# Three 64-byte-row loads ahead of the first store, and that store in one DMA instead of two

## The chip, the cores and the metric

The kernel runs on one core of one Trainium2 chip. The metric is the device time of an execution in microseconds (us). Before the change the median of three runs is 314.12 us (314.10 to 314.14).

## What is computed

Two arrays are woven into one along the last axis, in 32-bit floats. Each input has 32 x 256 x 1024 elements (33.55 MB), the output twice that (67.11 MB).

```python
result = np.zeros((batch, seq, dim * 2), dtype=np.float32)
result[..., 0::2] = x
result[..., 1::2] = y
```

Nothing is computed on the values. All 134.22 MB have to pass through the core's 16 DMA engines once: 67.11 MB are read and 67.11 MB are written.

## The kernel before, in words

`x` and `y` are cut into n = 8 tiles each, numbered k. A tile is 128 partitions (rows of the on-chip memory) by W = 8192 elements, so a row is 32 KiB and a tile is 4 MiB. The output tile k is twice as wide; it is written in two halves h = 0 and 1, each again 128 rows of 32 KiB, from a buffer of its own. Below, "store [k,h]" is the DMA of half h of tile k. There are two buffers each for x (`xt`), for y (`yt`) and for the output halves (`ot`).

Four parts run side by side and meet at semaphores:

- **Loads**, on the queue of SyncE (SP): x0 in two halves (the second half goes out on the other queue, L46), then y0, x1, y1, x2, y2 and so on (L45 to L55). From k = 2 on, the load of x into a buffer waits until VectorE has copied the x of tile k-2 out of it (L50), and the load of y the same for y (L54).
- **Weaving**, on VectorE (DVE): per half, one copy puts half a tile of x into the even elements of `ot[h]` (L67) and one copy puts y into the odd ones (L70). The x copy waits for the load of x and, through `osem[h]` (L66), for the store that last used `ot[h]`. The first y copy of a tile waits for the load of y. Each copy raises `woven` by one.
- **Stores**, on the queue of ScalarE (ACT): when both copies of a half are done (L74), the half goes out (L76). Store [0,0] alone is cut in two by `parts` (L39): its first quarter goes as 128 rows of 8 KiB, the rest as 128 rows of 24 KiB. `stored` (L42) counts the increments that `osem` has then got. ACT does nothing else but issue these.
- **The end**: ACT waits for the last store of half 0 and clears the semaphores (L80, L83); SP waits for the last store of half 1 (L84).

A DMA is spread over the 16 DMA engines; with 128 rows each engine gets 8 of them. Each engine keeps the rows of the two queues apart, and adds to each DMA's rows a packet of 4 bytes that raises the semaphore. `tile_interleave_kernel` moves the first DMA of either queue into the program's opening; that touches the two halves of x0 only.

Of the kernel before, what the change touches and what calls it, by code (L numbers as in the profile page):

```python
# [3 lines left out]


def _interleave(nc, x, y, out):
    P = 128
    W = 8192
    H = W // 2  # L10

    total = 1
    for s in x.shape:
        total *= s
    n = total // (P * W)
    assert n * P * W == total

    def rows(ap, names, k):
        flat = ap.rearrange("b s d -> (b s d)")
        return flat[k * names : (k + 1) * names].rearrange("(p w) -> p w", p=P)  # L20

    fp32 = mybir.dt.float32
    xt = [nc.alloc_sbuf_tensor(f"xt{b}", [P, W], fp32).ap() for b in (0, 1)]
    yt = [nc.alloc_sbuf_tensor(f"yt{b}", [P, W], fp32).ap() for b in (0, 1)]
    ot = [nc.alloc_sbuf_tensor(f"ot{b}", [P, W], fp32).ap() for b in (0, 1)]

    xsem = [nc.alloc_semaphore(f"xsem{b}") for b in (0, 1)]
    hsem = nc.alloc_semaphore("hsem")
    ysem = [nc.alloc_semaphore(f"ysem{b}") for b in (0, 1)]
    woven = nc.alloc_semaphore("woven")  # L30
    osem = [nc.alloc_semaphore(f"osem{b}") for b in (0, 1)]

    xs = [rows(x, P * W, k) for k in range(n)]
    ys = [rows(y, P * W, k) for k in range(n)]
    os_ = [rows(out, 2 * P * W, k) for k in range(n)]

    Q = W // 4

    def parts(k, h):  # L39
        return [slice(0, W)] if k or h else [slice(0, Q), slice(Q, W)]  # L40

    def stored(k, h):  # L42
        return 16 * sum(len(parts(j, h)) for j in range(k))

    nc.sync.dma_start(out=xt[0][:, :H], in_=xs[0][:, :H]).then_inc(xsem[0], 16)  # L45
    nc.scalar.dma_start(out=xt[0][:, H:], in_=xs[0][:, H:]).then_inc(hsem, 16)  # L46
    for k in range(n):
        b = k % 2
        if k >= 2:
            nc.sync.wait_ge(woven, 4 * (k - 2) + 3)  # L50
        if k:
            nc.sync.dma_start(out=xt[b], in_=xs[k]).then_inc(xsem[b], 16)
        if k >= 2:
            nc.sync.wait_ge(woven, 4 * (k - 2) + 4)  # L54
        nc.sync.dma_start(out=yt[b], in_=ys[k]).then_inc(ysem[b], 16)  # L55

    for k in range(n):
        b = k % 2
        for h in (0, 1):
            c = slice(h * H, (h + 1) * H)  # L60
            if h == 0:
                nc.vector.wait_ge(xsem[b], 16 * (k // 2 + 1))
            elif k == 0:
                nc.vector.wait_ge(hsem, 16)
            if k:
                nc.vector.wait_ge(osem[h], stored(k, h))  # L66
            nc.vector.tensor_copy(out=ot[h][:, 0::2], in_=xt[b][:, c]).then_inc(woven, 1)  # L67
            if h == 0:
                nc.vector.wait_ge(ysem[b], 16 * (k // 2 + 1))
            nc.vector.tensor_copy(out=ot[h][:, 1::2], in_=yt[b][:, c]).then_inc(woven, 1)  # L70

    for k in range(n):
        for h in (0, 1):
            nc.scalar.wait_ge(woven, 4 * k + 2 * h + 2)  # L74
            for c in parts(k, h):
                nc.scalar.dma_start(  # L76
                    out=os_[k][:, h * W : (h + 1) * W][:, c], in_=ot[h][:, c]
                ).then_inc(osem[h], 16)

    nc.scalar.wait_ge(osem[0], stored(n, 0))  # L80
    used = sorted(s.num for s in [*xsem, hsem, *ysem, woven, osem[0]])
    assert used == list(range(used[0], used[-1] + 1)), used
    nc.scalar.sem_clear(range(used[0], used[-1] + 1))  # L83
    nc.sync.nop(nofuse=True).wait_op(osem[1], stored(n, 1), "sem-ge").then_inc(  # L84
        osem[1], -stored(n, 1)
    )


def kernel(tc, x, y, out):
    nc = tc.nc  # L90
    tc.close()
    tc.compile()

    _interleave(nc, x, y, out)

    blocks = nc.main_func.blocks
    for engine in (mybir.EngineType.SP, mybir.EngineType.Activation):
        opening = blocks[0].instructions
        at, moved = next(
            (b, i)  # L100
            for b in blocks[1:]
            for i in b.instructions
            if i.engine == engine and i.opcode == "DMACopy"
        )
        assert not (moved.sync_info and moved.sync_info.on_wait)
        body = at.instructions
        body.remove(moved)
        gate = next(
            n
            for n, i in enumerate(opening)  # L110
            if i.engine == engine and i.opcode == "Drain"
        )
        opening.insert(gate, moved)
        at.instructions = body
        blocks[0].instructions = opening


# [1 line left out]
_INS = ['x', 'y']  # L119
_OUTS = [((32, 256, 2048), 'float32')]  # L120


# [23 lines left out]
```

## Time and profile before

| | |
|---|---|
| median of the runs | 314.12 us |
| the profiled execution | 314.21 us |
| its span, from the first to the last instruction | 312.9 us |
| read and written | 67.11 MB and 67.11 MB, 429 GB/s over the span |
| packets | 4896, of which 544 are under 512 bytes (34 DMAs x 16 engines) |
| DMA queue of ACT (q10), of SP (q1) | 51.3% and 48.5% of the 16 engines' span |
| VectorE busy | 71.9 us (23%), 32 copies of some 2.29 us |
| issue of the first store | at 24.35 us |
| landing of store [0,0] | first DMA at 40.41 us, second at 57.50 us |
| last load lands | 277.78 us |
| last four stores land | 283.80, 293.49, 303.18 and 312.85 us |

The profile is of one execution. The span leaves 1.33 us outside the first and the last instruction. The profile's page names the queue of SP q1 and that of ACT q10. "Share of 16 engines" is the time that the packets of a queue took, against 16 times the length of the span or of the stretch that was asked for; the two queues' shares together show how full the DMA engines were. A landing is the moment at which the last of the 16 engines has raised the DMA's semaphore. The trace also holds a record of each packet: its start, its length, its size and its queue, but not its engine.

### The profile page before, as it was taken

How to read it: one execution, taken by the hardware profiler on the slowest of the kernel's cores; microseconds unless marked ns; L12 is line 12 of the kernel's file. 1: busy time of each engine (PE TensorE's matmuls, PEld its weight loads, DVE VectorE, ACT ScalarE, POOL GpSimd, SP SyncE). 2: the span in 40 equal slices, each digit the busy share in tenths (PEclk: the TensorE clock that was granted, in tenths of full speed). 3: DMA queues.
4: the chain of work that ended last, by engine and by line, in shares of the span. 5: the costliest groups of instructions: out<-in, count | busy, mean ns of one | idle time of the engine just before them, and what ended most of it. 6: DMA issues, size and time to landing. Idle time of an engine off the chain costs nothing.

```text
span 312.9 us, 114 instructions
## 1 busy us (share of the span) xinstructions
DVE 71.9 (23%) x32; POOL 0.2 (0%) x4
## 2 busy tenths in 40 slices
DVE  0216000501305023050230503205032050415400
POOL 0000000000000000000000000000000000000000
DMA  8999999999999999999999999999999999999998
GB/s 344 461 406 431 436 402 431 440 465 406 448 423 431 440 406 465 402 469 402 469 402 465 406 457 415 436 436 419 452 402 469 402 469 402 469 402 461 411 444 360
DMA packets 4896, 134.22 MB, mean 429 GB/s; under 512 B 544, under 2 KB 544, under 8 KB 544
## 3 DMA queue, kind: packets, MB, share of 16 engines
q10 hardware_dynamic: 2592, 69.21, 51.3%
q1 hardware_dynamic: 2304, 65.01, 48.5%
HBM read 67.11 MB, written 67.11 MB: 429 GB/s over the span
## 4 chain that ended last, share of the span: by engine, by line
DMA 82%; DVE 12%; issue 0%
DMA out_dram<-ot 76%; DMA yt<-in_y_dram 7%; DVE ot L70 6%; DVE ot L67 6%
## 5 line engine op out<-in xcount | busy, mean ns | idle before, releaser
L67 DVE COPY ot<-xt 128x4096 f32<-128x4096 f32 x16 | 36.7, 2295 | 218.0 <-DMA out_dram<-ot 206.3
L70 DVE COPY ot<-yt 128x4096 f32<-128x4096 f32 x16 | 36.6, 2288 | 8.0 <-DMA yt<-in_y_dram 8.0
L130 POOL MEMSET const-uint8-127<- 128x1 uint8 x1 | 0.1, 102 | 0.0
L130 POOL MEMSET const-bfloat16-1.0<- 128x1 bf16 x1 | 0.1, 101 | 0.0
L130 POOL MEMSET const-float32-0.0<- 128x1 f32 x1 | 0.1, 98 | 0.2 <-issue 0.2
L130 POOL MEMSET const-float32-1.0<- 128x1 f32 x1 | 0.1, 98 | 0.0
## 6 DMA issues: line engine op xcount, KB each, us to landing
out_dram<-ot ACTq DMA_DIRECT2D x15, 4096.0 KB, 34.1
yt<-in_y_dram SPq DMA_DIRECT2D x8, 4096.0 KB, 41.5
xt<-in_x_dram SPq DMA_DIRECT2D x7, 4096.0 KB, 24.4
out_dram<-ot ACTq DMA_DIRECT2D x1, 3072.0 KB, 32.8
xt<-in_x_dram SPq DMA_DIRECT2D x1, 2048.0 KB, 11.7
xt<-in_x_dram ACTq DMA_DIRECT2D x1, 2048.0 KB, 13.4
out_dram<-ot ACTq DMA_DIRECT2D x1, 1024.0 KB, 16.1
```

The costliest lines, as they stand in the source:

```text
L67: nc.vector.tensor_copy(out=ot[h][:, 0::2], in_=xt[b][:, c]).then_inc(woven, 1)
L70: nc.vector.tensor_copy(out=ot[h][:, 1::2], in_=yt[b][:, c]).then_inc(woven, 1)
L130: nc = _bacc.Bacc("TRN2", target_bir_lowering=False, num_devices=1)
```

## The change

Store [0,0] becomes one DMA with rows of 32 KiB, as all others are. Ahead of it, on the same queue and behind the same wait for the first two copies, ACT issues three loads of 4, 8 and 12 rows of 64 bytes from the start of x into a spare tile that nobody reads. They raise a semaphore of their own, `tsem`, for which ACT waits at the end. The increments in `osem` are counted without the extra part.

```diff
+    spare = nc.alloc_sbuf_tensor("spare", [12, 48], fp32).ap()
...
+    tsem = nc.alloc_semaphore("tsem")
...
-    def parts(k, h):
-        return [slice(0, W)] if k or h else [slice(0, Q), slice(Q, W)]
-
-    def stored(k, h):
-        return 16 * sum(len(parts(j, h)) for j in range(k))
...
-                nc.vector.wait_ge(osem[h], stored(k, h))
+                nc.vector.wait_ge(osem[h], 16 * k)
...
-            for c in parts(k, h):
-                nc.scalar.dma_start(
-                    out=os_[k][:, h * W : (h + 1) * W][:, c], in_=ot[h][:, c]
-                ).then_inc(osem[h], 16)
+            if k == h == 0:
+                for r in (4, 8, 12):
+                    nc.scalar.dma_start(
+                        out=spare[:r, slice(4 * r - 16, 4 * r)],
+                        in_=xs[0][:r, slice(4 * r - 16, 4 * r)],
+                    ).then_inc(tsem, 16)
+            nc.scalar.dma_start(
+                out=os_[k][:, h * W : (h + 1) * W], in_=ot[h]
+            ).then_inc(osem[h], 16)
...
+    nc.scalar.wait_ge(tsem, 48)
```

More of the change, by code (lines that the diff above doesn't have):

```diff
@@ L35, in _interleave @@
     os_ = [rows(out, 2 * P * W, k) for k in range(n)]
-    Q = W // 4
-    def parts(k, h):
-        return [slice(0, W)] if k or h else [slice(0, Q), slice(Q, W)]
-    def stored(k, h):
-        return 16 * sum(len(parts(j, h)) for j in range(k))
     nc.sync.dma_start(out=xt[0][:, :H], in_=xs[0][:, :H]).then_inc(xsem[0], 16)
@@ L74, in _interleave @@
             nc.scalar.wait_ge(woven, 4 * k + 2 * h + 2)
-            for c in parts(k, h):
-                nc.scalar.dma_start(
-                    out=os_[k][:, h * W : (h + 1) * W][:, c], in_=ot[h][:, c]
-                ).then_inc(osem[h], 16)
-    nc.scalar.wait_ge(osem[0], stored(n, 0))
-    used = sorted(s.num for s in [*xsem, hsem, *ysem, woven, osem[0]])
+            if k == h == 0:
[8 more added lines that the diff above has]
+    nc.scalar.wait_ge(tsem, 48)
+    nc.scalar.wait_ge(osem[0], 16 * n)
+    used = sorted(s.num for s in [*xsem, hsem, tsem, *ysem, woven, osem[0]])
     assert used == list(range(used[0], used[-1] + 1)), used
     nc.scalar.sem_clear(range(used[0], used[-1] + 1))
-    nc.sync.nop(nofuse=True).wait_op(osem[1], stored(n, 1), "sem-ge").then_inc(
-        osem[1], -stored(n, 1)
+    nc.sync.nop(nofuse=True).wait_op(osem[1], 16 * n, "sem-ge").then_inc(
+        osem[1], -16 * n
     )
```

## The prediction

> **What bounds the kernel.** I read the page first, then the rate stage by stage, then the packet records around the first store.
>
> The slices of the page and its chain of waits:
>
> ```profile
> DMA  8999999999999999999999999999999999999998
> DMA packets 4896, 134.22 MB, mean 429 GB/s; under 512 B 544, under 2 KB 544, under 8 KB 544
> ...
> DMA 82%; DVE 12%; issue 0%
> ```
>
> The DMA engines are full in every slice but the first and the last. The chain names VectorE for 12%, but only because it follows waits: the digits show that the DMA engines stay busy while VectorE copies. The bound is therefore not the chain but the 16 engines' throughput. The table by stretches says how flat it is, with one whole period of the loop per line (start and end, length, VectorE, GpSimd, clock, DMA share, GB/s):
>
> ```profile
> 77.00:115.70 38.70, 8.96 (x5) 0.00 (x0) 1.00 1.00 434
> 115.70:154.40 38.70, 8.97 (x5) 0.00 (x0) 1.00 1.00 434
> 154.40:193.20 38.80, 9.06 (x5) 0.00 (x0) 1.00 1.00 432
> ```
>
> Per engine a period is 32 rows of 32 KiB. The packet records give 1213 ns for nearly each of them, load or store; 32 x 1.213 = 38.8 us. So the middle cannot be quickened by another order of the same rows. Time is lost only where an engine has no row, or a row takes over 1213 ns.
>
> There are two such places. The start: the first packet begins at 1.00 us and the first 16 take 1.27 us on average where later ones of their size take 0.61. The change does not touch it. The other is where the stores begin. The DMA view of two stretches, 13.5 to 26.9 us (loads alone) and then 27.0 to 32.1 us (first store rows):
>
> ```profile
> q1 hardware_dynamic: 192, 5.77, 99.6%
> ```
> ```profile
> q1 hardware_dynamic: 48, 1.57, 80.6%
> q10 hardware_dynamic: 42, 0.34, 15.9%
> ```
>
> In the first, 0.996 x 13.4 us x 16 engines over 176 rows (16 of the 192 are 4-byte packets) is 1.213 us a row; in the second, 0.806 x 5.1 x 16 / 48 = 1.371 us. Three load rows per engine are each 0.158 us too long: **0.47 us lost per engine**. It ends at 32.2 us; from 60 us on nothing of the kind comes back.
>
> How an engine shares itself between the queues is seen from 28.45 to 40.85 us, while store [0,0] sends its 8 KiB rows:
>
> ```profile
> DMA packets 288, 5.24 MB, mean 423 GB/s; under 512 B 32, under 2 KB 32, under 8 KB 32
> ...
> q1 hardware_dynamic: 144, 4.19, 81.4%
> q10 hardware_dynamic: 144, 1.05, 20.0%
> ```
>
> Both queues got 144 packets, 9 per engine: 8 rows and one 4-byte packet each. The engine changes queue after every packet, whatever its size, and the 4-byte packet (9 ns) uses a turn. Whoever sends short packets lets the other queue go ahead.
>
> **The change, part by part.** Times are against the profiled execution, 314.21 us, span 312.9.
>
> *The split goes.* A row pair cost 309 + 912 = 1221 ns; one row of 32 KiB costs 1213. That is 8 ns x 8 rows, and one completion packet of 9 ns less: **-0.07 us** per engine. It counts in full, since every engine is full to the end. On ACT one issue of 0.34 us goes.
>
> *What the split did to the order goes too.* It cost the store queue 9 more turns, so loads ran ahead. Now loads get fewer rows before the stores become equal. At 28.5 us, when the first store row started, an engine had 22 of its 128 load rows done. Alternating from there (106 pairs of 2.426 us) it ends its loads at 285 us (sem packets and the later start move that up to 288) instead of 277. Some 22 store rows then remain, 22 x 1.213 = 26.7 us, which is the same end: 312. Order changes, sums do not.
>
> *Three loads come.* Each engine that gets a row of such a load has two more packets per load on the store queue (row and completion), so two turns in which a 32 KiB load row passes. With one row per engine, the engine that takes part in all three sees 6 turns, 6 x 1.213 = 7.3 us; engines that take part in none go on at once. The stores of some engines thus run up to 7.3 us behind, and their loads as far ahead. By the section "Why a DMA increments its semaphore by 16 and not by 1" of the Trainium skill's page "DMA: Bandwidth & Descriptors", 4, 8 and 12 rows go to the 4, 8 and 12 lowest engines, which would give lags of 6, 4, 2 and 0 turns; the trace has DMAs of 128 rows only, all with 16 completions, and cannot show it.
>
> Their own time: 64 bytes lie between the rows of 4 bytes (9 ns) and 8 KiB (309 ns). The records fall nearly on a line (309, 611, 1213), so I take 9 ns: 6 x 9 = **+0.05 us** on the engine with all three. From below it cannot be less than nothing. From above, a packet whose read is not fetched ahead: the first 16 rows took 0.66 us more than later ones on average, at most 0.97 (1.58 against 0.61); 3 x 0.97 = +2.9 us. I take the low end, because the nearest case is the second half of x0, the first load on the ACT queue beside a running SP queue: its first 16 rows took 619 to 721 ns against 611, so the read of a first packet is fetched while another packet runs.
>
> *Issues on ACT.* Three more at 0.34 to 0.46 us put the first store off by about 1.1 us (24.35 to 25.4). Store [0,1] waits for copies that end at 28.7, so nothing else moves. The cover is x1 and y1, 10 load rows per engine at 28.5 us; without it 1.1 us would be lost.
>
> *Does an engine run dry?* Store [0,0] lands on the lagging engine at about 28.5 + 7.3 + 8 x 2.426 = 55.2 us (before: 57.50). y1 lands on the leading one about 52 to 55. Copies (4.5 us) end near 60, and store [1,0] goes out. The engines furthest ahead still have [0,1] until 29.7 + 16 x 2.426 = 68.5. From issue to first packet the first store took 28.5 - 24.35 = 4.1 us, so 4 us are to spare, and a dry store queue would only let loads pass. In the last stretch both matter: [6,1] ends with 16 rows left, 312.5 - 19.4 = 293.1. y7 lands at 285 to 288, its copy (2.3 us) lets [7,0] go at 287 to 290.3; that leaves 2.8 us or more, where the fastest issue to first packet is 1.0 (first load). By then loads are over on all engines and the lag is made up.
>
> *The 0.47 us at the first stores.* Not explained by the trace. Bounds: it goes (-0.47), or it lasts for the six extra load rounds as well (6 x 0.158 = +0.95). I take 0, the row as it is.
>
> *The added wait on `tsem`* stands at the end of ACT, long after those loads. Nothing.
>
> Sum: 314.21 - 0.07 + 0.05 = 314.19. The median of the runs lies 0.09 below the profiled execution, so the forecast is **314.1 us**.
>
> **Against it: the fixed cost of a DMA.** The last rows in store order end at 303.18 and 312.85 us with 9.67 us between them, 8 x 1.213 = 9.70: no gap between one DMA and the next. The same page ("Anatomy of one DMA") gives about 2 us of fixed cost per DMA, which for two more DMAs would be an estimated +4 us, 318; the trace shows that cost hidden behind the other rows, so the rule stands only beside the third rival.
>
> **The rivals.**
> 1. *The loss at the first stores disappears* because the engines no longer begin together: 314.19 - 0.47 - 0.09 = 313.6. For it: it sits in a lockstep start. Against: lockstep rows from 33 us on lose nothing. Chance 0.12, of which 0.05 reaches past -0.2%.
> 2. *It lasts or grows* with the longer staggered start: up to 315.0. Chance 0.08, half of it past +0.2%.
> 3. *The small loads are not hidden* (the slower side). Place: the engine with all three; each read makes the store queue's turn idle for 0.66 to 0.97 us: 2.0 to 2.9, so 316 to 317. It decides from 0.2 us each, since every delay of a full engine shows at the end. Chance 0.08.
> 4. *The rows of one small load go to one engine*: 24 rows and 3 completions, 27 turns, 33 us of lag there. Store [0,0] would land near 80 us; the others have 26 load and 16 store rows from 28.5 us on, until 79.5, and idle until [1,0] goes out about 87: some +8, 322. It decides when the lag exceeds the 16 store rows' slack. Chance 0.03.
> 5. *The margin before [7,0] is lost*, as with the 4.1 us of the first store against 2.8: +1.3, 315.4. Chance 0.03.
>
> **How the numbers follow.** The forecast has 0.66. A difference under 0.2% (0.63 us) is what a measurement of this kernel can tell from no change. Faster: 0.05 from rival 1 and 0.02 from elsewhere, 0.07. Slower: 0.04 + 0.08 + 0.03 + 0.03, 0.18. The same: 0.75. The range takes in the ends of rivals 1 and 2, 313.5 to 315.2; rivals 3, 4 and 5, 0.14 together, lie above it.
>
> **What would show it.** Packets 4896 - 144 + 48 = 4800, under 512 bytes 544 - 16 + 48 = 576; the periods still at 434 GB/s. Store [0,0] lands at 52 to 57 us; the completions of one DMA spread over some 7 us instead of 0.34 until the loads end, then join again. The last load at 285 to 288. Rows over 1213 ns around 28 to 36 us tell rivals 1 and 2; a DMA share under 1.00 between 280 and 300 tells 5; a hole around 80 us tells 4. The forecast is wrong if an engine shows a gap anywhere after 36 us.

## The result: slower by 0.34%

The changed kernel takes 315.11 us in the median of 6 runs (314.85 to 315.99), the kernel before 314.13 (314.10 to 314.29). The ratio is 1.0034, with a 95% interval of 1.0022 to 1.0046. The time lies inside the forecast's range (313.5 to 315.2), but the forecast was "no change" with 0.75, and "slower" had 0.18. It also varies more from run to run than before: over 1.1 us instead of 0.2. In the ratios below, executions more than 1.5% above the fastest of their kernel are left out (one each of e4 and e9); the medians hold them.

The profiled execution took 314.86 us with a span of 313.5 us (before: 314.21 and 312.9). The slices, the packets and the chain of its page:

```profile
DMA  8999999999999999999999999999999999999997
GB/s 337 466 401 418 401 451 406 464 406 464 406 460 406 464 406 464 406 464 406 456 414 452 418 451 418 435 435 414 456 406 464 406 460 406 464 406 464 406 464 339
DMA packets 4800, 134.22 MB, mean 428 GB/s; under 512 B 576, under 2 KB 576, under 8 KB 576
...
DMA 82%; DVE 12%; issue 0%
```

The page hardly differs: the same full slices, the same chain. 4800 packets with 576 small ones are what the change asks for. Three whole periods in the middle (stretch, length, VectorE, GpSimd, clock, DMA share, GB/s):

```profile
73.60:112.30 38.70, 8.99 (x4) 0.00 (x0) 1.00 1.00 434
112.30:151.00 38.70, 8.99 (x4) 0.00 (x0) 1.00 1.00 434
151.00:189.70 38.70, 8.99 (x4) 0.00 (x0) 1.00 1.00 433
```

Nothing was lost there either. What is left is the beginning of the stores. The DMA view from 27.0 to 32.1 us, the stretch that showed 80.6% and 15.9% before:

```profile
q1 hardware_dynamic: 67, 1.84, 99.7%
q10 hardware_dynamic: 47, 0.23, 10.9%
```

The shares sum to over 100% because rows that run past the stretch count whole, so the rows have to be read one by one. The packet records carry no engine, but rows follow one another without a gap and each engine gets a known number of packets from each DMA, so the records can be strung into 16 sequences. In each I sum by how much rows exceed their usual length (1213 ns for 32 KiB, 309 for 8, 611 for 16, 912 for 24) from 20 us on. I call that the engine's **loss**. Before: 0.53 us on average, 0.32 to 0.68. After: 0.92 on average, **0.58 to 1.23**. Single load rows between 28.5 and 33 us take up to 2193 ns.

The loss has become larger, and also unequal. That is seen at the end, where each engine's last packet raises a semaphore. The DMA view from 312.6 us on, first of the kernel before, then of the changed one:

```profile
DMA packets 0, 0.00 MB, mean 0 GB/s; under 512 B 0, under 2 KB 0, under 8 KB 0
```
```profile
DMA packets 15, 0.00 MB, mean 0 GB/s; under 512 B 15, under 2 KB 15, under 8 KB 15
```

Before, all engines are done by then (312.17 to 312.50 us); after, 15 of 16 still have their last packet to send (312.52 to 313.16). The time of the kernel is that of the last engine, plus 1.70 us in nearly every profile of this study.

### The profile page after: what moved, and what is told of

It is laid out like the page before. It is cut to its first block, busy times and chain, and to the rows that moved or that the text cites. A ratio compares the mean times of both kernels' runs of the same rounds, so it can differ in the third digit from the quotient of the medians.

```text
span 313.5 us, 117 instructions
## 1 busy us (share of the span) xinstructions
DVE 72.0 (23%) x32; POOL 0.2 (0%) x4
## 4 chain that ended last, share of the span: by engine, by line
DMA 82%; DVE 12%; issue 0%
DMA out_dram<-ot 76%; DMA yt<-in_y_dram 7%; DVE ot L65 6%; DVE ot L62 6%
## 6 DMA issues: line engine op xcount, KB each, us to landing
xt<-in_x_dram ACTq DMA_DIRECT2D x1, 2048.0 KB, 13.5
```

## The experiments

All times are medians. What a kernel is "above before" is its distance from the kernel before measured beside it on the same chip, 314.20 to 314.24 us; the row "before" is of the comparison above. Loss and last end are of the one profiled execution, whose time is in the fourth column.

| kernel | median (runs) | ratio, 95% interval | profiled | loss: mean, most | last engine ends |
|---|---|---|---|---|---|
| before | 314.13 | | 314.21 | 0.53, 0.68 | 312.50 |
| after | 315.11 (6) | 1.0034, 1.0022 to 1.0046 | 314.86 | 0.92, 1.23 | 313.16 |
| e1 unsplit, no small loads | 314.47 (11) | 1.0008, 0.9999 to 1.0016 | 314.52 | 0.86, 1.09 | 312.82 |
| e2 split and small loads | 316.29 (6) | 1.0064, 1.0042 to 1.0087 | 314.94 | 0.93, 1.30 | 313.25 |
| e3 early touch | 316.54 (5) | 1.0070, 1.0057 to 1.0083 | 317.04 | 2.00, 3.57 | 315.34 |
| e4 x2 and y2 held | 317.44 (6) | 1.0096, 1.0074 to 1.0118 | 317.88 | 1.81, 4.42 | 316.16 |
| e5 all sixteen | 314.49 (12) | 1.0005, 0.9995 to 1.0015 | 314.43 | 0.73, 0.85 | 312.73 |
| e6 small loads early | 314.25 (12) | 0.9996, 0.9986 to 1.0006 | 314.29 | 0.60, 0.88 | 312.60 |
| e7 small loads mid | 314.21 (12) | 0.9998, 0.9990 to 1.0006 | 314.22 | 0.53, 0.82 | 312.51 |
| e8 one of eight | 315.15 (11) | 1.0035, 1.0021 to 1.0049 | 317.14 | 1.81, 3.35 | 315.43 |
| e9 small loads second | 321.62 (6) | 1.0232, 1.0189 to 1.0275 | 325.07 | 3.28, 11.31 | 323.36 |
| e10 large part first | 314.40 (11) | 1.0005, 0.9996 to 1.0013 | 314.40 | 0.55, 1.04 | 312.69 |
| e11 two halves | 314.42 (11) | 1.0006, 0.9997 to 1.0015 | 314.40 | 0.60, 0.77 | 312.71 |
| e12 three-part ramp | 315.09 (11) | 1.0029, 1.0017 to 1.0040 | 315.46 | 0.59, 1.82 | 313.76 |
| e13 mended | 318.88 (6) | 1.0148, 1.0115 to 1.0181 | 317.55 | 1.67, 4.03 | 315.84 |
| e14 sixteen, second | 314.53 (11) | 1.0012, 1.0003 to 1.0021 | 314.53 | 0.72, 0.84 | 312.83 |
| e15 after, second profile | 315.06 (1) | | 315.06 | 0.96, 1.38 | 313.23 |
| e16 after, third profile | 315.61 (1) | | 315.61 | 1.16, 2.22 | 313.77 |

**Which part of the change.** e1 drops the small loads, e2 puts them into the kernel before.

```diff
# e1, against the changed kernel
-            if k == h == 0:
-                for r in (4, 8, 12):
...
# e2, against the kernel before
             nc.scalar.wait_ge(woven, 4 * k + 2 * h + 2)
+            if k == h == 0:
+                for r in (4, 8, 12):
...
```

> The changed kernel without the three small loads: store [0,0] is one DMA of 32 KiB rows, all engines begin it together. Theory A (the small loads are to blame: they make the engines begin to store one group after the other, and the loads that still run are slowed for as long as that lasts): 314.0 to 314.2 us as before, loss between 26 and 40 us about 0.5 us per engine. Theory B (the longer rows of the first store are to blame, the small loads are innocent): 314.9 to 315.2, loss about 0.9. If both count, something between.

> The kernel before with the three small loads ahead of its two-part first store. Theory A: 314.8 to 315.2 us, with the loss around the first stores at 0.9 us. Theory B: 314.1 to 314.3 us, loss 0.5.

e1 is 0.23 us above before, and its interval just reaches no change; e2 is 2.05 us above. The small loads count far more than the split. In e1 all engines lose more than before (0.67 to 1.09). Two kernels further down that also begin with an unsplit store in step, e5 and e14, are 0.29 and 0.32 us above with a mean loss of 0.73, and e14's interval excludes no change; so the unsplit store most likely costs some 0.2 to 0.3 us. How far the loss accounts for it is open: e9, the same as e1 up to its second store, lost only 0.53 before 50 us.

In these four the loss has a place. All their rows that are over 0.03 us too long before 50 us are load rows that begin before any engine's first store row: in e1 the store is issued at 24.21 us, the long rows begin from 25.81 to 27.87, the first store row at 29.1.

Whether the split also harms beside the small loads is not shown. The intervals of e2 and of the changed kernel overlap, and the profile of e2 is of its fastest execution. It has no load row from 81.4 to 86.9 us: its load queue ran dry, as that of the changed kernel never did before the loads ended.

**What the loss is not.** e3 writes to the output early; e4 issues fewer DMAs near the first store.

```diff
# e3
+    nc.scalar.wait_ge(xsem[0], 16)
+    nc.scalar.dma_start(out=os_[0][:, :16], in_=xt[0][:, :16]).then_inc(wsem, 16)
+    nc.scalar.wait_ge(wsem, 16)
...
# e4
             nc.sync.wait_ge(woven, 4 * (k - 2) + 3)
+            if k == 2:
+                nc.sync.wait_ge(osem[0], 16)
```

> The changed kernel; in addition 128 rows of 64 bytes go from the first x tile to the 128 rows of the first output tile as soon as x0's first half is there (some 12 us), and the first store overwrites them. Theory C (the loss comes with the first write to the output, whoever makes it): the loss moves to some 13 to 17 us or goes, and there is none at 28 to 36 us; if it goes, 314.1 us or below. Theories A and B: loss and time as in the changed kernel, 314.9 to 315.5.

> The changed kernel; SP issues the loads of x2 and y2 only after store [0,0] has landed (some 54 us), so that fewer DMAs are issued from 24 to 29 us. Theory D (the loss comes from the many DMA issues in those microseconds): the loss at 28 to 36 us shrinks to under 0.4 us per engine, 314.2 to 314.5. Theories A, B and C: loss about 0.9, 314.9 to 315.5. The queue of SP may be empty for a moment near 54 us, which costs nothing while stores run.

In e3 no row is too long from 12 to 27 us, while the early rows are written, and from 27 to 36 us an engine loses 0.76 us on average. In e4 it is 0.89 there, in the changed kernel 0.90. The first write (theory C) and the burst of issues (theory D) are out. Both kernels turned out slower by losses further on. In e3, whose first store goes out 1.0 us later, the eight engines with two or three small loads lose another 1.4 to 2.6 us each after 60 us, the others at most 0.9. In e4 the four engines with two small loads have store rows up to 1.25 us too long at 40 to 46 us and, as the held loads begin, at 55 to 58; they lose 4.2 to 4.4 us in all, the others up to 1.4. e4 also shows what the prediction's fifth rival would look like. Its timeline near the end:

```profile
282.71 2.29 DVE L64 COPY ot<-xt 128x4096 f32<-128x4096 f32 x1 [14.93 <-DMA out_dram<-ot]
292.34 2.29 DVE L67 COPY ot<-yt 128x4096 f32<-128x4096 f32 x1 [7.33 <-DMA yt<-in_y_dram]
294.67 7.38 ACTq L78 DMA_DIRECT2D out_dram<-ot  x2
```

y7 comes late, store [7,0] goes out at 294.67 us, its first rows start at 295.51, and twelve engines stand still for 1.8 to 2.4 us. In the changed kernel the same copy ends at 289.27 us, and [6,1] lands at 293.50 to 294.17: no gap.

**Together or in groups.** e5 gives every engine the same extra turns; e6 and e7 put the small loads elsewhere; e8 keeps one load, so two groups 2 turns apart.

```diff
# e5, against the changed kernel
-                        out=spare[:r, ...], in_=xs[0][:r, ...]
+                        out=spare[:16, ...], in_=xs[0][:16, ...]
# e6, against the kernel before: the three loads right behind the load of x0's second half
# e7, against the kernel before
+            if k == 3 and h == 0:
+                for r in (4, 8, 12):
...
# e8, against the changed kernel
-                for r in (4, 8, 12):
+                for r in (8,):
```

> The changed kernel with 16 rows in each of the three small loads, so that all engines get the same 6 extra turns and begin to store together, as much later as the last ones in the changed kernel. Theory A (staggering costs): the completions of a store lie within 0.7 us, time as in the unsplit kernel without small loads, 0.1 to 0.4 us above the kernel before. Theory F (six more turns at the start of the stores cost, whoever has them): 0.9 us or more above it, as in the changed kernel.

> The kernel before, with the three small loads right behind the second half of x0 on the ACT queue, about 12 us before any store is ready. The stagger is then gone before the stores begin, since the ACT queue is empty from some 20 us on. Theory A: within 0.15 us of the kernel before. If the small loads cost by themselves (reads of 64 bytes, issues, three more completions): 0.5 us or more above it.

> The kernel before, with the three small loads ahead of store [3,0] (issued near 139 us) instead of the first store. Theory A in its wide form (engines out of step cost whenever they fall out of step): no loss before 140 us beyond that of the kernel before, rows over 1213 ns behind it, 0.4 us or more above the kernel before. Theory G (only the beginning of the stores is touchy, a stagger later is free): within 0.15 us of the kernel before.

> The changed kernel with the load of 8 rows alone: two groups of engines, 2 turns (2.4 us) apart, instead of four groups over 6 turns. Theory A: between the unsplit kernel without small loads and the changed kernel, 0.3 to 0.8 us above the kernel before. Theory F: one third of the changed kernel's surplus. If two groups cost as much as four, the size of the stagger is not what counts.

e5 carries 48 small rows instead of 24 and is 0.29 us above before, no worse than e1 without any. e6 is 0.05 above. So neither the small loads nor the extra turns cost anything that these runs can tell: **putting engines out of step does.** Two groups (e8) cost as much as four, 0.95 us.

The medians carry this, not single executions: beside e5 to e8 the kernel before ranged from 314.09 to 315.59 us in 34 executions. The profile of e8 is of one of 317.14 us; its ten others took 314.93 to 315.76.

e7 cost nothing (0.01 us), but it is a weaker test than it was meant to be. In its records the engines that fell behind send three store rows in a row soon after: the load queue ran dry there, since in the kernel before x and y go out only some microseconds before the queue is empty. The completions of a store spread over 1.2 us at 174 us and 0.3 again at 212. It shows that being out of step for a short time costs nothing that can be told, no more.

**Beginning or for good.** e9 lets all engines begin together and puts them out of step one store later; e14 is its control with 16 rows in each load.

```diff
# e9, against the changed kernel; e14 the same with 16 rows each
-            if k == h == 0:
+            if k == 0 and h == 1:
```

> The changed kernel with the three small loads ahead of store [0,1] instead of [0,0]: all engines begin to store together, and fall out of step some 20 us later, when both queues are in turn. Theory H (what costs is that groups of engines begin to store one after the other; each beginning slows all engines once): loss before 60 us as in the unsplit kernel without small loads, 0.75 to 0.85 us per engine, and 0.15 to 0.45 us above the kernel before. Theory I (what costs is that the engines stay out of step for the rest): 0.8 us or more above it, with rows over 1213 ns after 60 us or a wider spread at the end.

> The kernel of e9 (small loads ahead of store [0,1]) with 16 rows in each of the three loads, so that no engine falls out of step. Theory I: the 7 us of e9 go, 0.2 to 0.4 us above the kernel before, completions of a store within 0.7 us. If six turns ahead of the second store cost by themselves (loads that run ahead or dry, x2 and y2 in another place): 2 us or more.

e9 is the strongest result of the study: 7.4 us, all but 0.3 of it from the stagger, since e14 is 0.32 us above before. Its six executions took 319.88 to 325.07 us, and its profile is of the slowest. There, from 59 us to some 200 us, up to four engines at a time lose 0.2 to 0.77 us in many of their rows. Their group can be told from the packets: an engine has 33 DMAs x 9 = 297, and two more for each small load that it takes part in. The four with 301, those with two small loads, lose 9.5 to 10.6 us each after 60 us; the other twelve, with none, one or three, at most 0.26. These four send their last packet at 321.9 to 323.4, the others at 319.8 to 320.0. The DMA view from 321.5 us on holds their four last packets and three of their rows:

```profile
DMA packets 7, 0.10 MB, mean 43 GB/s; under 512 B 4, under 2 KB 4, under 8 KB 4
```

The engines with two small loads are also those that lose most in e4, in e13 and in e16, a profile of the changed kernel. It is no rule: in e2 and e8 engines without any small load lose most.

The completions of one store spread over 6 us at 73 us and over 13.5 at 198. The two stretches below are a period and the last stores, first e9, then e14:

```profile
77.00:115.70 38.70, 5.09 (x3) 0.00 (x0) 1.00 1.00 424
...
294.00:310.00 16.00, 8.99 (x4) 0.00 (x0) 1.00 0.72 307
```
```profile
77.00:115.70 38.70, 8.96 (x5) 0.00 (x0) 1.00 1.00 434
...
294.00:310.00 16.00, 4.34 (x2) 0.00 (x0) 1.00 1.01 438
```

In the middle e9's DMA engines seem just as full (1.00), but move 2% less: rows are longer, not missing. At the end 0.72 shows engines that stand still, since VectorE must wait for the slow ones before it can fill the next output half.

e13 was to keep the staggered beginning and to bring the engines back into step near 50 us.

```diff
# e13, against the changed kernel
         nc.sync.dma_start(out=yt[b], in_=ys[k]).then_inc(ysem[b], 16)
+        if k == 1:
+            for r in (4, 8, 12):
+                nc.sync.dma_start(out=mend[:r, ...], in_=xs[0][:r, ...]).then_inc(msem, 16)
```

> The changed kernel; SP puts three loads of the same shape behind y1, so that each engine that fell behind in stores by 2, 4 or 6 turns gets as many turns back near 50 us. The staggered beginning stays, the engines are in step from some 60 us on. Theory H (the staggered beginning costs): the surplus of the changed kernel stays, 0.7 to 1.0 us above the kernel before. Theory I (being out of step for the rest costs): it falls to that of the unsplit kernel, 0.2 to 0.4 us.

It failed in its aim. The completions of a store still spread over some 3 us afterwards, so the engines were in another stagger, not in step; it cost 4.7 us. In its profile the four engines with two small loads on each queue lose 1.1 to 2.4 us after 60 us, the others up to 0.9, and ten engines stand still for 0.3 to 0.8 us before store [7,0]. It decides nothing between theories H and I, but it is one more pattern out of step that costs.

Two more profiles of the changed kernel itself:

> The changed kernel once more, for a second profile. Theory H: rows over 1213 ns between 26 and 36 us only, as in its first profile (0.6 to 1.2 us per engine), whatever its time. Theory I: a slower execution than 314.86 us has rows over 1213 ns, or engines that fall further behind, after 60 us.

> The changed kernel a third time, as in e15: the same two expectations. With both it is seen whether the loss before or after 60 us sets the time.

The last engine ends at 313.16, 313.23 and 313.77 us, the times are 314.86, 315.06 and 315.61. In all three it is one of the four engines with 301 packets. In the third profile those four have 1.39 to 1.85 us of loss before 60 us and up to 0.37 just behind, the other twelve 0.65 to 1.25 in all. The DMA view of the third profile from 312.95 us on:

```profile
DMA packets 4, 0.00 MB, mean 0 GB/s; under 512 B 4, under 2 KB 4, under 8 KB 4
```

Four last packets, of those four engines; twelve engines are done. From 66 us on none of the three profiles has a load or store row more than 0.03 us too long. So in the changed kernel the surplus arises between 27 and 66 us (theory H), most of it at the staggered beginning; the lasting loss of theory I is real in e3, e9, e13 and the profile of e8, and not seen here, in executions of up to 315.61 us.

**What the split is for.** e10, e11 and e12 change the parts of the first store in the kernel before.

```diff
-        return [slice(0, W)] if k or h else [slice(0, Q), slice(Q, W)]
+        ... else [slice(0, 3 * Q), slice(3 * Q, W)]                       # e10
+        ... else [slice(0, 2 * Q), slice(2 * Q, W)]                       # e11
+        ... else [slice(0, Q // 4), slice(Q // 4, Q), slice(Q, W)]        # e12
```

> The kernel before with its two-part first store the other way round: rows of 24 KiB first, then rows of 8 KiB. Theory J (the beginning of the stores costs by the length of the first store row): loss between 26 and 36 us about 0.6 to 0.8 us per engine, 0.1 to 0.3 us above the kernel before. Theory K (the split helps since it costs the store queue nine more turns, which lets the loads run ahead): as the kernel before, within 0.1 us.

> The kernel before with the first store cut into two halves of 16 KiB rows. Theory J: loss of 0.5 to 0.7 us per engine, 0.0 to 0.2 us above the kernel before. Theory K: as the kernel before, within 0.1 us.

> The kernel before with the first store in three parts, rows of 2, 6 and 24 KiB. Theory J: the loss at the first rows falls under 0.3 us per engine, that at the first rows of 24 KiB (0.1 to 0.3) stays; up to 0.3 us under the kernel before. Theory K: as the kernel before, or slower if the loads, 9 more turns ahead, run dry.

Rows of 8 KiB first: the kernel before. 16: 0.19 us more, 24: 0.17, 32 (e1): 0.23. e10 costs the store queue the same 9 turns as the split of before, and still is slower; that speaks, weakly, against theory K: these intervals just reach no change. Nor does it settle for J: J asked for a loss of 0.6 to 0.8 us in e10, and its mean is 0.55, as good as the 0.53 of before. The times follow the first row; the loss does so only in part. The ramp (e12) has hardly a loss at its 2 KiB rows, as J has it; the loss moved to 49 us, where the rows of 24 KiB begin. It is slower all the same, by 0.86 us. Its load queue runs dry, which is theory K's case for a slower kernel: there is no load row from 72.9 to 87.0 us. The DMA view from 75 to 82 us has the store queue alone:

```profile
DMA packets 111, 3.11 MB, mean 445 GB/s; under 512 B 16, under 2 KB 16, under 8 KB 16
...
q10 hardware_dynamic: 111, 3.11, 103.0%
```

At 87.34 us, as the loads begin again beside running stores, one store row is 0.50 us too long; from 105 us on some engines are out of step (one load's completions spread over 2.3 us, later 2.8), and the last one ends at 313.76 us where the others end at 312.1 to 312.9. No kernel of the study beats the one before.

## Why the prediction was wrong

**The step that failed** is "The 0.47 us at the first stores. Not explained by the trace. ... I take 0, the row as it is." Two things were wrong in it. The size: it became 0.92 us on average; its bounds were drawn from the row of before alone. The longer first rows had no price in them, and the stagger only that of six more rounds. And the way it was counted: an average over engines, where the slowest engine sets the end. In step, the loss is shared almost alike (0.32 to 0.68 before); staggered, it was 0.58 to 1.23, 0.61 to 1.38 and 0.65 to 2.22 us in three profiles. The sixteen last packets say what that is worth. Their mean end is 312.30 us before and 312.76, 312.77 and 312.90 after; the last one is 0.19 us behind the mean before and 0.40, 0.46 and 0.87 behind it after. So all engines together end 0.5 to 0.6 us later, and the inequality adds 0.2 to 0.7. By the runs, the unsplit store alone brings 0.23 of the 0.98 us (e1) and the small loads the other 0.75 on top of it; with the split left in (e2) the small loads bring 2.05, so these two shares hold in this order only.

The lag itself, 6, 4, 2 and 0 turns, was computed and, beyond that bound, taken as free ("Order changes, sums do not"). e9 shows that such a lag can cost 7 us.

**Rival 2** ("lasts or grows") is the case that came, with 0.08. Its price of 315.0, and the range that held the result, were near the mark by luck: the loss did not go on through six more rounds. But for one row it ends at 34 us, after about as many rounds as before; single load rows are up to 0.98 us too long instead of 0.38.

**Rival 1 did not come:** the engines no longer began together, and the loss grew. Being in step was not its cause; it kept the loss alike on all engines. The reading of the loss before stopped early: nine more load rows are too long from 39.7 to 42.2 us, where the rows of 24 KiB begin, so the whole is 0.53 us and not 0.47.

**What was right.** The turns: the completions of one store spread over 5.25 us and join to 0.67 when the loads are over. I had 7.3: the engines ahead begin a turn later than I took (30.55 us), and x1's completion packet fills one of the six extra turns, so the last begin at 35.6. Packets, periods, the landing of store [0,0] (54.22 us, forecast 52 to 57), the last load (286.45, forecast 285 to 288) and the margin before [7,0] came as computed. A 64-byte row took 11 ns (I had 9); rival 3 is out, as e5 and e6 confirm. The section "Anatomy of one DMA" of the Trainium skill's page "DMA: Bandwidth & Descriptors", from which the prediction has its 2 us per DMA, fits them to DMAs issued from GpSimd, and these come from SyncE and ScalarE. Here three more DMAs (e5 against e1) cost 0.06 us. The lags follow the section "Why a DMA increments its semaphore by 16 and not by 1" of the Trainium skill's page "DMA: Bandwidth & Descriptors": e16 has four engines each with 297, 299, 301 and 303 packets, so 12, 8 and 4 rows went to 12, 8 and 4 engines, which rules out rival 4. The records can't say which engines these are.

**What stays open:** why load rows grow just ahead of the first store rows, why in so many of these kernels the engines with two small loads lose most, and why the same lag is nearly harmless from the first store on and costs 7 us from the second. The runs show where and how much, not by what.

## What to carry to other kernels

When all DMA engines are full to the end, judge a change of the DMA order by the last engine, not by the mean share: through their middle, e9 and e14 had the same DMA share of 1.00 and are 7 us apart. Small transfers on few engines cost next to nothing in bytes and time, but each packet, the completion too, takes a turn on those engines alone; put them where the queue is otherwise empty (e6), or give them 16 rows (e5, e14). Short rows in the first store after a stretch of loads are worth some 0.2 us here, at the edge of what these runs can tell.

## What was not expected of the hardware

- Of engines out of step a few can be slowed for 140 us, by up to 0.77 us in a row of 1.213, with the DMA share at 1.00 throughout (e9). It was the four with two small loads; those with none, one or three lost at most 0.26 us.
- When stores begin after a stretch of loads alone, load rows grow, in step only those ahead of the first store row, staggered also later ones: by up to 0.38 us with 8 KiB store rows, up to 0.83 with 32 KiB rows in step (e1), up to 1.42 staggered (e16). Rows of 2 KiB raise hardly any (e12).
- From the issue of a store to its first rows, with nothing else queued on those engines, e4 shows 0.84 us (294.67 to 295.51), and e9 and e13 the same (299.50 to 300.34, 293.15 to 293.99); with load rows ahead it was 4.1 in the kernel before.
